# Queues of VectorE and ScalarE in order of use, in all stages of seven products, and the second sums of weights behind the first splits

## The chip, the core and the metric

The kernel runs on one core of one Trainium2 chip. The metric is the device time of one execution in microseconds. TensorE (PE) multiplies, VectorE (DVE), ScalarE (ACT) and GpSimd (POOL) prepare operands and take results away, SyncE (SP) issues most of the loads. Each engine works through its own queue in the order in which the program put its instructions there, and waits on semaphores for the others.

## What is computed

One decoder layer for 512 tokens of width 2048 in float32: an input projection shared by three groups of heads, the heads themselves, an output projection, and a feed-forward layer of width 8192.

```python
xn = rms_norm(h, attn_norm_g)
proj = xn @ w_in
...
o = jnp.concatenate([gla_o, fox_o, mem_o], axis=2)
o = rms_norm(o, out_norm_g.reshape(N_OUT_HEADS, HEAD_DIM)).reshape(B, S, -1)
gate = jnp.concatenate([jax.nn.silu(gg), jax.nn.sigmoid(fg), jax.nn.sigmoid(mg)], axis=-1)
h = h + (o * gate) @ w_out

u = jax.nn.relu(rms_norm(h, mlp_norm_g) @ w_up)
h = h + (u * u) @ w_down
```

## The kernel before

**A product in float32.** Each operand is split into a high half in the type fp32r (ScalarE casts, `A.copy`) and a low half, the remainder (VectorE subtracts). `mm3` (L157 to L159) multiplies high by high, high by low and low by high.

**Seven products.** Part of the input projection and the whole output, up and down projections multiply blocks of two by two by the scheme with seven products in place of eight. `ORDER` is 1, 5, 6, 3, 7, 2, 4. Products 1, 2 and 3 take a raw block of the weight or one that is used as it was loaded, products 5, 6, 7 and 4 take sums of blocks. `multiply` (L337) runs the seven products for one set of weights (`Weights`). Of a set of the out, up and down stage each product has four steps q = 0 to 3 of 12 matmuls; a step is written (p, q) here. Of the input pairs (`Pair`) it has two steps. The out stage has two sets, up has eight groups, down has eight sets (four chunks of two).

**What a step needs.** `split(p, q)` makes the high and low half of 1024 columns of the weight, the tile `hl_..._pq`, in one of four buffers. At q = 0 it first calls `prepare` for both halves s of the block: the load of the next raw block (tiles `raw_..._rcs`, 2048 columns) by SyncE, and the sum of 2048 columns for products 5, 6, 7 and 4 by VectorE (in the input pairs GpSimd makes the sums of 7 and 4). So both sums of a product stand ahead of its first split. All that stands under a priority of `AHEAD`, and the scheduler places the instructions in the queues by it.

**Left operands.** `left0` to `left6` hold the seven sums of the activations, as high half (h) and low half (l; of S2 the last quarter is `left4m`). For the out stage, `gate(3)` makes the last quarter of these sums behind the attention heads: A11 and S1 are split at once (`left0`, `left3`), the others go through memory (`oo_i`) by GpSimd's DMAs and are loaded again by `fetch` and split by `resplit` (L1280). For down, `renew` loads and splits those of the next chunk while the current one runs.

**Evictions.** At the end of a product `after` takes the accumulators away, under the priority `urgent` (2 x AHEAD): in the input pairs into `o` (ScalarE L451 or VectorE L449), in out into `x` (VectorE L1217), in up into `z` (ScalarE copies L1356, or VectorE adds and ScalarE's relu L1316), in down into `m` (ScalarE L1400). From `z` the up stage makes transposes `ut` on TensorE (L1301) and squares `u` (L1302).

**First sets.** The weights of out0 and up0 are marked `lead`; their first eight steps run in the order (1,0), (1,1), (1,2), (5,0), (5,1), (5,2), (1,3), (5,3). `x_sums(0)` makes the sums of x for the input pairs from the tiles `xs`, and `qTs`, `kTs` (L373, L374) copy projections out of the banks in which `ss_x` (the sum of squares of x, L207) is then made.

## Time and profile before

| | us |
|---|---|
| median of 3 runs | 2146.14 (2144.59 to 2147.57) |
| the profiled execution | 2146.72 |
| its span | 2145.0 |

The stages of seven products lie in the span about so: input pairs 98 to 260 us, out 704 to 874, up 874 to 1517, down from 1517 to the end. Between the input pairs and out are the other projections and the heads. The granted clock of TensorE is 0.998 over the span.

A row of the profile names the engine, the line, the operation, the tile written and the tiles read (out<-in, buffer numbers left out), the shape, and for groups the count; "idle before" is the time for which the engine did nothing ahead of it, with what ended that.

### The profile page before, as it was taken

To read this page: it belongs to the slowest core of one execution; us is meant where nothing else is said; L and a number is where in the kernel's file an instruction comes from. 1 tells how busy PE (TensorE), PEld (TensorE's weight loads), DVE (VectorE), ACT (ScalarE), POOL (GpSimd) and SP (SyncE) were. 2 spreads that over 40 slices of the span, in tenths; PEclk is the share of its full clock that TensorE was granted. 3 is DMA by queue.
4 is the path that set the end of the run, shared out by engine and by line. 5 is a ranking of instruction groups with operands and counts; after the bars stand their busy time and mean duration, and the time that the engine had idled before them with its cause. 6 is when DMAs were issued, how large, how long until landed. Compare 5 with 4: busy or idle time off the path is not lost.

```text
span 2145.0 us, 25543 instructions
## 1 busy us (share of the span) xinstructions
PE 2104.4 (98%) x9746; PEld 1732.6 (81%) x9746; DVE 1615.4 (75%) x1723; ACT 1134.3 (53%) x1603; POOL 191.7 (9%) x236
## 2 busy tenths in 40 slices
PE   8999999999999899999999999999999999999999
PEld 7877778887888788788888888888788788788787
DVE  7679897773664988977777777778867767877875
ACT  6554464434554655655555555556546546556543
POOL 0252200000000021100000000000100000000000
PEclk9999999999999999999999999999999999999999
DMA  7544342121233675253353353356578568668653
GB/s 264 168 138 139 98 149 85 60 69 59 84 105 136 230 268 205 92 196 128 135 192 128 141 189 132 134 190 232 170 203 245 159 192 258 170 183 276 174 166 130
DMA packets 78755, 347.09 MB, mean 162 GB/s; under 512 B 9305, under 2 KB 13401, under 8 KB 57130
## 3 DMA queue, kind: packets, MB, share of 16 engines
q1 hardware_dynamic: 58778, 274.95, 36.9%
q0 software_dynamic: 19856, 70.53, 12.5%
q8 instruction: 76, 1.25, 0.2%
q14 instruction: 45, 0.37, 0.1%
HBM read 271.52 MB, written 73.92 MB: 161 GB/s over the span
## 4 chain that ended last, share of the span: by engine, by line
PE 80%; DVE 9%; DMA 6%; issue 3%; ACT 2%; POOL 1%; SPq 0%; ACTq 0%; DVEq 0%; POOLq 0%
PE acc_up L157 9%; PE acc_up L158 9%; PE acc_up L159 9%; PE acc_dn L158 7%; PE acc_dn L159 7%; PE acc_dn L157 7%; PE acc_out L158 2%; PE acc_out L157 2%; PE acc_out L159 2%; DMA left1l<-op 2%; DVE hl_dn L334 2%; PE gg L157 1%; PE gg L159 1%; PE gg L158 1%; DVE raw_dn L296 1%
## 5 line engine op out<-in xcount | busy, mean ns | idle before, releaser
L334 DVE TENSOR_TENSOR hl_up<-raw_up,hl_up 128x1024 fp32r<-128x1024 f32 x224 | 271.6, 1222 | 142.7 <-ACT hl_up L334 142.5
L334 ACT CAST hl_up<-raw_up 128x1024 fp32r<-128x1024 f32 x224 | 235.7, 1054 | 254.0 <-PE acc_up L159 194.0
L334 DVE TENSOR_TENSOR hl_dn<-raw_dn,hl_dn 128x1024 fp32r<-128x1024 f32 x224 | 270.5, 1222 | 103.9 <-ACT hl_dn L334 103.3
L334 ACT CAST hl_dn<-raw_dn 128x1024 fp32r<-128x1024 f32 x224 | 235.0, 1055 | 206.5 <-PE acc_dn L159 164.5
L296 DVE TENSOR_TENSOR raw_dn<-raw_dn,raw_dn 128x2048 f32<-128x2048 f32 x64 | 146.1, 2287 | 15.1 <-DMA raw_dn<-in_w_down_dram 14.9
L296 DVE TENSOR_TENSOR raw_up<-raw_up,raw_up 128x2048 f32<-128x2048 f32 x64 | 145.1, 2267 | 2.0 <-DMA raw_up<-in_w_up_dram 1.9
L1401 POOL DMA_DIRECT2D hd<-m x48 | 41.6, 866 | 514.4 <-ACT m L1400 514.4
L334 ACT CAST hl_out<-raw_out 128x1024 fp32r<-128x1024 f32 x56 | 58.6, 1053 | 52.8 <-PE acc_out L159 40.1
L334 DVE TENSOR_TENSOR hl_out<-raw_out,hl_out 128x1024 fp32r<-128x1024 f32 x56 | 69.0, 1253 | 15.1 <-ACT hl_out L334 15.0
L1400 ACT COPY m<-acc_dn 128x512 f32<-128x512 f32 x96 | 54.6, 587 | 31.8 <-PE acc_dn L159 31.8
L1293 POOL DMA_DIRECT2D op<-u x32 | 17.1, 535 | 491.5 <-ACT u L1302 484.1
L158 PE MATMUL acc_dn<-hl_dn,left 128*128 128x512 f32 x128 | 50.3, 393 | 6.1 <-DVE hl_dn L334 6.1
L158 PE MATMUL acc_in<-hl_hl_in,sh 128*128 128x512 f32 x128 | 50.5, 395 | 5.4 <-DVE hl_hl_in L334 5.4
L157 PE MATMUL acc_up<-hl_up,left 128*128 128x512 f32 x128 | 50.6, 396 | 3.1 <-ACT z L1356 3.1
L157 PE MATMUL gg<-ahi_x,hl_gg 128*128 128x512 f32 x128 | 53.6, 418 | 0.0
L334 DVE TENSOR_TENSOR hl_hl_in<-spare,hl_hl_in 128x1024 fp32r<-128x1024 f32 x31 | 44.0, 1430 | 11.5 <-ACT hl_hl_in L334 11.4
L157 PE MATMUL acc_in<-hl_hl_in,sh 128*128 128x512 f32 x128 | 50.0, 390 | 1.3 <-ACT o L451 1.3
L158 PE MATMUL acc_dn<-hl_dn,left0h 128*128 128x512 f32 x128 | 50.0, 391 | 1.1 <-DVE hl_dn L334 1.1
L334 ACT CAST hl_hl_in<-spare 128x1024 fp32r<-128x1024 f32 x31 | 32.4, 1049 | 34.8 <-DVE spare L430 14.6
L157 PE MATMUL acc_up<-hl_up,left0h 128*128 128x512 f32 x128 | 50.5, 394 | 0.0
L157 PE MATMUL acc_up<-hl_up,left5h 128*128 128x512 f32 x128 | 50.5, 394 | 0.0
L157 PE MATMUL acc_up<-hl_up,left1h 128*128 128x512 f32 x128 | 50.5, 394 | 0.0
(545 smaller groups left out, 6277.1 us busy)
## 6 DMA issues: line engine op xcount, KB each, us to landing
raw_up<-in_w_up_dram SPq DMA_DIRECT2D x64, 1024.0 KB, 4.9
raw_dn<-in_w_down_dram SPq DMA_DIRECT2D x64, 1024.0 KB, 6.3
hd<-m POOLq DMA_DIRECT2D x48, 512.0 KB, 5.5
raw_out<-in_w_out_dram SPq DMA_DIRECT2D x16, 1024.0 KB, 5.3
op<-u POOLq DMA_DIRECT2D x32, 512.0 KB, 3.3
op<-s POOLq DMA_DIRECT2D x24, 512.0 KB, 3.5
spare<-in_w_pair_dram SPq DMA_DIRECT2D x16, 512.0 KB, 4.2
raw_in<-in_w_pair_dram SPq DMA_DIRECT2D x16, 512.0 KB, 4.3
```

Of the source, the lines that this page charges most:

```text
L157: T.matmul(ps, lhsT=ah, rhs=bh, start=start, stop=False, skip_group_check=on)
L158: T.matmul(ps, lhsT=ah, rhs=bl, start=False, stop=False, skip_group_check=on)
L159: T.matmul(ps, lhsT=al, rhs=bh, start=False, stop=stop, skip_group_check=on)
L296: V.tensor_sub(dst, a, b)
L334: made = A.copy(hi, part), V.tensor_sub(lo, part, hi.bitcast(F32))
L1293: nc.gpsimd.dma_start(down_op[c][i][:, half * 1024 : half * 1024 + 1024], tile)
L1400: A.copy(st[:, t * 512 : t * 512 + 512], acc[t])
L1401: nc.gpsimd.dma_start(dst, st.rearrange("p (t n) -> p t n", t=2), accum_op=ALU.add)
```

## The change

`turns["step"]` counts the steps. `empty` places an eviction under the high priority and remembers the last instruction of it on VectorE and on ScalarE; `behind(step)` puts what is issued in it behind the evictions up to that step. A split is now placed behind the evictions of four steps before, and behind the split that was made before it (`turns["made"]`), so splits stand in their order of use. `prepare` falls into `load_next` (both loads, at q = 0) and `sums`: the sum for half s is placed at q = s, that is, the second directly before split q = 1, and behind the evictions of eight steps before. The first sum of product 7 follows the last split of 5, that of 4 the last split of 7.

In the lead sets the sums of product 6 are cut into four pieces of 1024 columns, each before its split. For out0 the left operands that were loaded again are split at given steps (`in_turn`), in pieces of 512 or 1024 columns in the same chain as the weights. `gate(3)` gives its sums in three parts with different priorities, and its temporary tiles have other tags (buffers). In up0 the normalisation `rstd` is computed at step (6, 1), not (1, 1).

```diff
 
-    turns = dict(group=0, hl=0, raw=0)
+    turns = dict(group=0, hl=0, raw=0, step=0, made=())
+
...
+    def empty(evict, p, acc):
+        traced = nc.cur_bb.bb.instructions
+        last = traced[-1]
+        with tc.high_priority(offset=2 * AHEAD):
+            evict(p, acc)
+        start = next(i for i in reversed(range(len(traced))) if traced[i] is last) + 1
+        for engine in (V.engine, A.engine):
+            emptied.extend([(turns["step"], i) for i in traced[start:] if i.engine == engine][-1:])
+
+    def behind(step):
+
+        es = ExitStack()
+        for engine in (V.engine, A.engine):
+            for _, i in [e for e in emptied if e[0] <= step and e[1].engine == engine][-1:]:
+                es.enter_context(tc.issue_after(i))
+        return es
     spare = third.tile([128, 3584], F32, tag="third", name="spare")
...
-        def prepare(self, p, s):
+        def load_next(self, p):
+            if p in (1, 5, 6, 2):
+                to, r, c = {1: (self.t, 0, 0), 5: (self.b12, 0, 1), 6: (self.b22, 1, 1), 2: (self.b21, 1, 0)}[p]
+                to.extend([self.load(r, c, s) for s in range(2)])
+
+        def sums(self, p, s):
             t, b12, b22, b21 = self.t, self.b12, self.b22, self.b21
-            if p == 1:
-                t.append(self.load(0, 0, s))
-            elif p == 5:
-                b12.append(self.load(0, 1, s))
+            if p == 5:
                 cs = slice(0, 1024 if self.lead and s else self.per * 1024)
                 self.minus(p, t[s][:, cs], b12[s][:, cs], t[s][:, cs])
-            elif p == 6:
-                b22.append(self.load(1, 1, s))
+            elif p == 6 and not self.lead:
                 self.minus(p, t[s], b22[s], t[s])
             elif p == 7:
                 self.minus(p, b12[s], b22[s], b12[s])
-            elif p == 2:
-                b21.append(self.load(1, 0, s))
             elif p == 4:
                 self.minus(p, t[s], b21[s], t[s])
...
+            now = turns["step"]
             with tc.high_priority(offset=self.ahead if urgent else AHEAD):
                 if q == 0:
-                    for s in range(2):
-                        self.prepare(p, s)
+                    self.load_next(p)
+                if q < 2:
+                    with behind(now - 8) as es:
+                        last = (p, 0) if q else {7: (5, self.steps - 1), 4: (7, self.steps - 1)}.get(p)
+                        if self.lead and (p, q) == (7, 0):
+                            last = 6, 3
+                        if last:
+                            es.enter_context(tc.issue_after(self.parts[last][2][1].ins))
+                        self.sums(p, q)
                 blocks = {1: self.t, 5: self.t, 6: self.t, 4: self.t, 3: self.b22, 7: self.b12, 2: self.b21}[p]
                 raw = blocks[q // self.per]
-                if self.lead and (p, q) == (5, 3):
-                    cs = slice(1024, 2048)
-                    V.tensor_sub(raw[:, cs], self.b12[1][:, cs], raw[:, cs])
+                if self.lead and (p == 6 or (p, q) == (5, 3)):
+                    cs = slice(q % 2 * 1024, q % 2 * 1024 + 1024)
+                    b = self.b12 if p == 5 else self.b22
+                    with ExitStack() as es:
+                        if p == 6:
+                            es.enter_context(tc.issue_after((self.parts[6, q // 3][2][1] if q else seam[0]).ins))
+                        V.tensor_sub(raw[:, cs], b[q // 2][:, cs], raw[:, cs])
                 both = self.both(f"hl_{self.name}_{p}{q}")
                 hi, lo = both[:, :1024], both[:, 1024:]
                 at = q % self.per * 1024
                 part = raw[:, at : at + 1024]
-                made = A.copy(hi, part), V.tensor_sub(lo, part, hi.bitcast(F32))
+                with behind(self.first + 6 if self.lead and p == 6 else now - 4) as es:
+                    for i in turns["made"]:
+                        es.enter_context(tc.issue_after(i.ins))
+                    turns["made"] = made = A.copy(hi, part), V.tensor_sub(lo, part, hi.bitcast(F32))
             self.parts[p, q] = hi, lo, made
             return hi, lo, made
...
         chain = {}
+        w.first = turns["step"] + 1
         for p, q in steps:
+            turns["step"] += 1
             first = p in (1, 5, 2)
...
             if q == w.steps - 1:
-                after(p, acc)
+                with ExitStack() as es:
+                    if w.lead and p == 5:
+                        es.enter_context(tc.issue_after(seam[1].ins))
+                    after(p, acc)
 
...
     def in_pair(n, c):
+        def evict(p, acc):
+            r, col = WHERE[p]
+            for u in range(2):
+                t = 2 * r + u
+                dst = o[:, t, n * 1024 + col * 512 : n * 1024 + col * 512 + 512]
+                if c or p in (3, 7, 2):
+                    V.scalar_tensor_tensor(dst, acc[u], rs_x(t), dst, op0=ALU.mult, op1=ALU.add)
+                else:
+                    A.activation(dst, acc[u], AF.Copy, scale=rs_x(t))
+
         def after(p, acc):
-            r, col = WHERE[p]
-            with urgent():
-                for u in range(2):
-                    t = 2 * r + u
-                    dst = o[:, t, n * 1024 + col * 512 : n * 1024 + col * 512 + 512]
-                    if c or p in (3, 7, 2):
-                        V.scalar_tensor_tensor(dst, acc[u], rs_x(t), dst, op0=ALU.mult, op1=ALU.add)
-                    else:
-                        A.activation(dst, acc[u], AF.Copy, scale=rs_x(t))
+            empty(evict, p, acc)
...
         def temp(v):
-            tags = dict(s1="tb" if last else "bT", s2="td", s3="tb" if last else "eb", s4="td")
...
-        for i, src in block_sums(ot[:, :2, :256], ot[:, 2:, :256], ot[:, :2, 256:], ot[:, 2:, 256:], temp):
...
+        def keep_sums():
+            for i, src in block_sums(ot[:, :2, :256], ot[:, 2:, :256], ot[:, :2, 256:], ot[:, 2:, 256:], temp):
+                early = i in (A11, S1) or i == S2 and not last
+                if early and high:
+                    hi, lo = halves(high[i][:, cs]), halves(lower(i, cs))
+                    A.copy(hi, src)
+                    seam[:] = [V.tensor_sub(lo, src, hi.bitcast(F32))]
+                else:
+                    nc.gpsimd.dma_start(halves(out_op[i][:, cs]), src)
+                    if early:
+                        waiting.append((i, cs))
+                if i in (S2, S4):
+                    yield
...
+
+        sums = keep_sums()
+        next(sums)
+        return sums
 
     def place():
 
...
+    with tc.high_priority(offset=AHEAD):
+        next(sums)
+    with tc.high_priority(offset=AHEAD - 150):
+        next(sums)
 
...
                 nc.sync.dma_start(z[r, c].rearrange("p (t n) -> p t n", t=2), x[r, 2 * n + c])
 
+        def evict(p, acc):
+            for t in range(2):
+                v = z[WHERE[p]][:, t * 512 : t * 512 + 512]
+                V.tensor_add(v, v, acc[t])
+
         def after(p, acc):
             r, c = WHERE[p]
-            with urgent():
-                for t in range(2):
-                    v = z[r, c][:, t * 512 : t * 512 + 512]
-                    V.tensor_add(v, v, acc[t])
+            empty(evict, p, acc)
...
         def inside(p, q):
+            if not n and (p, q) == (5, 3):
+                first_operands()
+            if not n and p == 6 and q < 3:
+                w_first.split(3, q)
+                if q != 1:
+                    in_turn(S4, slice(512, 1536) if q == 0 else slice(1536, 2048))
+            if not n and q > 1 and p in (3, 7, 2):
+                for cs in ((slice(1024, 1536), slice(1536, 2048)) if q > 2 else (slice(0, 1024),)):
+                    in_turn({3: S3, 7: A12, 2: A22}[p], cs)
...
+    def in_turn(i, cs):
+
+        with ExitStack() as es:
+            es.enter_context(tc.high_priority(offset=AHEAD))
+            for m in turns["made"]:
+                es.enter_context(tc.issue_after(m.ins))
+            turns["made"] = split_left(i, cs, lower(i, cs).bitcast(F32))
+
+    def first_operands():
+        for q in range(4):
+            if q == 3:
+                in_turn(S2, slice(1536, 2048))
+            _, _, made = w_first.split(6, q)
+        seam.append(made[1])
+        in_turn(S4, slice(0, 512))
+
     def rest():
...
             with tc.high_priority(offset=1000):
                 fetch(i, cs, out_op[i][:, cs])
-            resplit(i, cs)
     for n in range(2):
         out_pair(n)
...
         def after(p, acc):
-            with urgent():
-                evict(p, acc)
+            empty(evict, p, acc)
...
                 rest()
-            if not g and (p, q) == (1, 1):
+            if not g and (p, q) == (6, 1):
```

The first place is ScalarE's queue between the copies of the query projection and the first input pair. `xs_1_951` and `xs_0_966` are the tiles xs_12_1 and xs_13_0 of x, `hl_hl_in_50` and `_51` splits (5,0) and (5,1). Before:

```order
L374 ACTIVATE qTs<-gq_111 128x4x128
L374 ACTIVATE qTs<-gq_112 128x4x128
L374 ACTIVATE qTs<-gq_113 128x4x128
L391 ACTIVATE xs_1_951<-xs_1_951,colt 128x512
L334 CAST hl_hl_in_51_1041<-spare 128x1024
L120 ACTIVATE y_x<-s_x 128x4
L374 ACTIVATE qTs<-gq_114 128x4x128
L391 ACTIVATE xs_0_966<-xs_0_966,colt 128x512
```

and after:

```order
L429 ACTIVATE xs_1_951<-xs_1_951,colt 128x512
L429 ACTIVATE xs_0_966<-xs_0_966,colt 128x512
L412 ACTIVATE qTs<-gq_111 128x4x128
L412 ACTIVATE qTs<-gq_112 128x4x128
L412 ACTIVATE qTs<-gq_113 128x4x128
L367 CAST hl_hl_in_51_1041<-spare 128x1024
L120 ACTIVATE y_x<-s_x 128x4
L412 ACTIVATE qTs<-gq_114 128x4x128
```

Both scalings of x tiles moved ahead of all four copies into qTs.

The second place is VectorE's queue in the first out set, from split (5,3) or the evictions of product 1 on. `x_00` and `x_11` are the residual blocks into which products 1 and 5 are evicted, `raw_out_00s` the raw blocks of which the sums for product 6 are made. Before:

```order
L334 TENSOR_TENSOR hl_out_53_5986<-raw_out_001_5744,hl_out_53_5986 128x1024
L334 TENSOR_TENSOR hl_out_60_6009<-raw_out_000_5742,hl_out_60_6009 128x1024
L296 TENSOR_TENSOR raw_out_001_5744<-raw_out_111_6006,raw_out_001_5744 128x2048
L334 TENSOR_TENSOR hl_out_61_6026<-raw_out_000_5742,hl_out_61_6026 128x1024
L296 TENSOR_TENSOR raw_out_010_5915<-raw_out_110_6003,raw_out_010_5915 128x2048
L1217 TENSOR_TENSOR x_00_5887<-x_00_5887,acc_out_1_0_5873 128x512
L1217 TENSOR_TENSOR x_00_5887<-x_00_5887,acc_out_1_1_5874 128x512
L1217 TENSOR_TENSOR x_11_5936<-x_11_5936,acc_out_5_0_5913 128x512
L1217 TENSOR_TENSOR x_11_5936<-x_11_5936,acc_out_5_1_5914 128x512
L334 TENSOR_TENSOR hl_out_62_6041<-raw_out_001_5744,hl_out_62_6041 128x1024
L334 TENSOR_TENSOR hl_out_63_6056<-raw_out_001_5744,hl_out_63_6056 128x1024
L296 TENSOR_TENSOR raw_out_011_5918<-raw_out_111_6006,raw_out_011_5918 128x2048
```

and after, from the first eviction:

```order
L1267 TENSOR_TENSOR x_00_5869<-x_00_5869,acc_out_1_0_5855 128x512
L1267 TENSOR_TENSOR x_00_5869<-x_00_5869,acc_out_1_1_5856 128x512
L367 TENSOR_TENSOR hl_out_60_5988<-raw_out_000_5742,hl_out_60_5988 128x1024
L359 TENSOR_TENSOR raw_out_000_5742<-raw_out_110_5983,raw_out_000_5742 128x1024
L359 TENSOR_TENSOR raw_out_001_5744<-raw_out_111_5985,raw_out_001_5744 128x1024
L367 TENSOR_TENSOR hl_out_61_5992<-raw_out_000_5742,hl_out_61_5992 128x1024
L359 TENSOR_TENSOR raw_out_001_5744<-raw_out_111_5985,raw_out_001_5744 128x1024
L367 TENSOR_TENSOR hl_out_62_5996<-raw_out_001_5744,hl_out_62_5996 128x1024
L582 TENSOR_TENSOR left4m<-left4m,left_5031 128x512
L367 TENSOR_TENSOR hl_out_63_6002<-raw_out_001_5744,hl_out_63_6002 128x1024
L1267 TENSOR_TENSOR x_11_5917<-x_11_5917,acc_out_5_0_5895 128x512
L1267 TENSOR_TENSOR x_11_5917<-x_11_5917,acc_out_5_1_5896 128x512
```

The evictions of product 1 moved ahead of split (6,0), split (5,3) is further ahead (five instructions stand between it and this piece), the sums of product 6 stand in pieces between its splits, the sum for product 7 (`raw_out_010`) has moved behind, and the low half of left4m stands before split (6,3).

The third place is ScalarE's queue at the first down set. `z_7_11396` (after: `z_7_11408`) is z4 of the last up group, `u_12` the square of its transpose, `hl_dn_0_pq` the splits. Before:

```order
L542 CAST left1h<-left1l 128x1024
L334 CAST hl_dn_0_12_11457<-raw_dn_0_001_11408 128x1024
L334 CAST hl_dn_0_13_11472<-raw_dn_0_001_11408 128x1024
L334 CAST hl_dn_0_50_11504<-raw_dn_0_000_11406 128x1024
L542 CAST left2h<-left2l 128x1024
L334 CAST hl_dn_0_51_11519<-raw_dn_0_000_11406 128x1024
L542 CAST left2h<-left2l 128x1024
L334 CAST hl_dn_0_52_11534<-raw_dn_0_001_11408 128x1024
L334 CAST hl_dn_0_53_11549<-raw_dn_0_001_11408 128x1024
L1316 ACTIVATE z_7_11396<-acc_up_1_0_10840,rstd 128x512
L1316 ACTIVATE z_7_11396<-acc_up_1_1_10841,rstd 128x512
```

and after:

```order
L582 CAST left1h<-left1l 128x1024 x2
L367 CAST hl_dn_0_12_11469<-raw_dn_0_001_11420 128x1024
L1394 ACTIVATE z_7_11408<-acc_up_1_0_10852,rstd 128x512
L1394 ACTIVATE z_7_11408<-acc_up_1_1_10853,rstd 128x512
L367 CAST hl_dn_0_13_11484<-raw_dn_0_001_11420 128x1024
L367 CAST hl_dn_0_50_11515<-raw_dn_0_000_11418 128x1024
L582 CAST left2h<-left2l 128x1024
L367 CAST hl_dn_0_51_11531<-raw_dn_0_000_11418 128x1024
L1380 ACTIVATE u_12_11452<-ut_12_0_11453 128x4x128
L1380 ACTIVATE u_12_11452<-ut_12_1_11459 128x4x128
L582 CAST left2h<-left2l 128x1024
```

The relu of z4 moved ahead of splits (1,3) and (5,0) and of both casts of left2, and the square of its transpose ahead of left2's second cast.

More of the change, by code (lines that the diff above doesn't have):

```diff
@@ L1127, in projections @@
             assert n in heads_of
[L1128 removed]
+            for _ in gate(n, ps):
+                pass
             yield
```

24 lines of the change are left out of this document (7 added, 17 removed).

## The prediction

> **What bounds the kernel now.** I read the page's shares first.
>
> ```profile
> span 2145.0 us, 25543 instructions
> PE 2104.4 (98%) x9746; PEld 1732.6 (81%) x9746; DVE 1615.4 (75%) x1723; ACT 1134.3 (53%) x1603; POOL 191.7 (9%) x236
> ```
>
> TensorE is busy 98% of the span. The change leaves its matmuls and transposes as they are, so it can win only what TensorE waits for, and what a wait does to the next matmuls. The view of waits, for TensorE, lists them all; these are the rows of the stages of seven products and of what stands around them (us in total, times, longest):
>
> ```profile
> PE acc_dn L158 <- DVE hl_dn L334: 7.3, 6, 1.8
> PE acc_in L158 <- DVE hl_hl_in L334: 5.4, 5, 1.5
> PE acc_up L157 <- ACT z L1356: 3.1, 1, 3.1
> PE acc_out L157 <- DVE x L1217: 3.1, 1, 3.1
> PE ut L1301 <- ACT z L1316: 2.7, 1, 2.7
> PE acc_out L158 <- DVE hl_out L334: 2.2, 2, 1.8
> PE acc_out L157 <- ACT left3h L1080: 1.9, 1, 1.9
> PE acc_in L157 <- ACT o L451: 1.3, 1, 1.3
> PE ss_x L207 <- ACT qTs L374: 1.1, 1, 1.1
> PE acc_in L157 <- DVE o L449: 0.7, 1, 0.7
> ```
>
> They add up to 28.8 us in some twenty places. Waits on the low half of a split (L158 <- DVE) come to 14.9 us; the others are waits for an eviction or for one operand, each once.
>
> A long wait costs more than itself: the granted clock falls behind it. The view by windows (us, PE busy, granted clock, DMA share, GB/s) shows the place:
>
> ```profile
> 728.00:734.00 6.00, 4.15 (x10) 0.72 0.72 234
> 734.00:743.00 9.00, 7.55 (x27) 0.81 0.97 349
> 902.30:905.70 3.40, 3.40 (x9) 0.50 0.00 0
> ```
>
> A window's length times the clock that is missing gives the loss: 6 x 0.28, 9 x 0.19 and 3.4 x 0.50, about 1.7 us each, 5.1 us in all. So **33.9 us** (28.8 + 5.1) is the most that the change can win in these stages, 1.6%.
>
> How far the splits run ahead elsewhere tells whether the steady part has anything to lose. From the page's costliest groups, and one whole group of the up stage from the windows:
>
> ```profile
> L334 ACT CAST hl_up<-raw_up 128x1024 fp32r<-128x1024 f32 x224 | 235.7, 1054 | 254.0 <-PE acc_up L159 194.0
> L334 DVE TENSOR_TENSOR hl_up<-raw_up,hl_up 128x1024 fp32r<-128x1024 f32 x224 | 271.6, 1222 | 142.7 <-ACT hl_up L334 142.5
> L296 DVE TENSOR_TENSOR raw_up<-raw_up,raw_up 128x2048 f32<-128x2048 f32 x64 | 145.1, 2267 | 2.0 <-DMA raw_up<-in_w_up_dram 1.9
> ```
>
> The casts there stand idle 194.0 us until TensorE frees one of four buffers, and VectorE idles 142.5 us for the casts: TensorE is the slowest of the three and the splits lean on their buffers. A step of TensorE is
>
> ```profile
> 720.67 0.39 PE L159 MATMUL acc_out<-hl_out,left3l 128*128 128x512 f32 x1
> ...
> 723.39 0.39 PE L159 MATMUL acc_out<-hl_out,left0l 128*128 128x512 f32 x1
> ```
>
> 12 matmuls later, 2.72 us. With four buffers a cast starts three steps ahead of its use, 8.2 us; less the cast (1.05) and the subtraction (1.22) the lead is at best 5.9 us.
>
> **The change, part by part.** The same instructions are issued but for 8 more on VectorE and 4 more on ScalarE, because some sums and operand splits are cut into pieces. Two pieces of 1024 columns take 2.35 us on VectorE where one of 2048 takes 2.28 (rows in (b)), so a cut adds about 0.07 us, nothing that counts. What matters is who stands before whom. I go by place.
>
> *(a) Input products, 98 to 260 us: +2.7 us.* On ScalarE two scalings of the x tiles, xs_12_1 and xs_13_0, now stand ahead of the copies qTs, for the first of which the statistics matmul ss_x waits.
>
> ```profile
> 93.88 1.59 ACT L391 ACTIVATE xs<-xs,colt 128x512 f32<-128x512 f32 x2 [6.17 <-DMA xs<-in_xT_dram]
> 96.31 1.56 ACT L374 ACTIVATE qTs<-gq 128x512 f32<-128x512 f32 x3
> 94.64 0.43 DVE L244 TENSOR_TENSOR st<-xs,xs 128x256 f32<-128x256 f32 x1 [2.60 <-ACT xs L391]
> 97.05 1.02 PE L207 MATMUL ss_x<-wide,xacc 128*128 128x1 f32 x8 [1.12 <-ACT qTs L374]
> DMA to landing us min/median/max: 2.8/3.4/3.6
> ```
>
> The two tiles take buffers that VectorE's sums of the tiles before them must release. The new order runs those four sums in a row from 94.64, 0.34 us each, so the last buffer is free at 96.0. The loads land 2.8 to 3.6 us later (98.8 to 99.6), the two scalings take 0.73 us each, qTs starts at 100.1 to 101.1 in place of 96.31, and ss_x follows 0.74 us behind it: +3.8 to +4.8, I take +4.1. Queued behind the two blocked scalings on ScalarE is, besides qTs, the cast of split (5,1), which TensorE needs only later. TensorE is then idle from about 95.9 to 101.2, longer than the wait ahead of the 0.50 window, so I add 1.3 us of slow clock (the idle time takes part of that window itself). Against this, TensorE arrives some 5 us later at everything behind, where VectorE, GpSimd and the evictions are not pushed back as far: the waits of 1.3 (o by ScalarE), 0.7 (o by VectorE) and the first of the five on a split (1.5) go, 3.5 us. Of the other four I expect +0.8, as GpSimd's second difference now stands before split (5,1) of the second pair. 4.1 + 1.3 - 3.5 + 0.8 = +2.7. Bounds: 0 (everything absorbed) and +5.5 (nothing).
>
> *(b) Output products, first pair, 704 to 760 us: -3.3 us.*
>
> ```profile
> 709.46 1.23 DVE L296 TENSOR_TENSOR raw_out<-raw_out,raw_out 128x1024 f32<-128x1024 f32 x1 [1.79 <-DMA raw_out<-in_w_out_dram]
> 721.09 0.68 DVE L1069 TENSOR_TENSOR o<-o,ee_mg 128x512 f32<-128x512 f32 x1
> 721.70 2.28 DVE L296 TENSOR_TENSOR raw_out<-raw_out,raw_out 128x2048 f32<-128x2048 f32 x1
> 723.90 1.29 DVE L244 TENSOR_TENSOR s_mg<-o 128x512 f32<-128x512 f32 x2
> 726.91 2.35 DVE L334 TENSOR_TENSOR hl_out<-raw_out,hl_out 128x1024 fp32r<-128x1024 f32 x2
> 734.72 2.47 DVE L1217 TENSOR_TENSOR x<-x,acc_out 128x512 f32<-128x512 f32 x4
> 737.40 0.62 ACT L542 CAST left<-left4m 128x512 fp32r<-128x512 f32 x1 [3.86 <-DMA left4m<-oo]
> ```
>
> Now: the whole 2048-wide difference at 721.70 and the gate's sums stand before split (5,3), which ends at 728.0; the evictions into x start at 734.72 behind five splits and sums. That is 1.9 + 1.8 + 3.1 of waits and 3.4 of slow clock, 10.0 us with TensorE. After: gate products fill VectorE's idle 1.79 us at 709.46, worth about 1.65 us; the step behind 721.70 then begins at 720.05 and runs gate sum (0.60), split (5,3) (1.14), left3l and a gate sum (1.20), half a difference (1.14), two gate sums, two evictions (2.40), split (6,0) (1.14): it ends at 727.7. Step (5,3) starts without a wait at 723.6 and ends at 726.3, so (6,0) waits 1.2 us at its second matmul. (6,1) has two half differences and a split before it, 3.4 us against a step of 2.72: 0.7. Before (6,3) the new queues of both engines put the cast and the low half of left4m, whose load landed at 737.40 here; if it lands between 735 and 737.4 (the store it needs comes no earlier, but the queue ahead of it changed), (6,3) waits 1.7 to 2.9 us: 2.3. VectorE is saturated, with the eviction of x_01 now ahead of (7,0): 2.5 for (7,0) and (7,1). New sum 6.7, gain 3.3. Bounds: 0 and 6.
>
> Here a rule of the Trainium skill can be held against the trace. The row 902.30:905.70 shows half clock for 3.4 us behind a wait of 3.1 us. The Trainium skill, "TensorE: Matmul & The Clock Gate", section "What's actually happening", says that the clock drops to half after at least one idle window of about 3.4 us and comes back after about 3.4 us of work. The length agrees with the row; the threshold doesn't, since a wait of 3.1 us, and two of 1.9 and 1.8 us in a row, sufficed. By the page none of the new waits of (b) would slow the clock and the term stays -3.3; by the trace a pair of them can, and it would be -1.6.
>
> *(c) Up products, first group, 890 to 906 us: -2.4 us.*
>
> ```profile
> 898.28 1.99 ACT L334 CAST hl_up<-raw_up 128x1024 fp32r<-128x1024 f32 x2 [3.82 <-DVE raw_up L296]
> 900.18 2.04 ACT L1356 COPY z<-acc_up 128x512 f32<-128x512 f32 x4
> 899.23 0.68 DVE L543 TENSOR_TENSOR left4m<-hs,left 128x512 fp32r<-128x512 f32 x1
> 899.83 1.22 DVE L334 TENSOR_TENSOR hl_up<-raw_up,hl_up 128x1024 fp32r<-128x1024 f32 x1
> 874.00:900.00 26.00, 23.59 (x107) 18.96 (x105) 26.00 (x23) 15.80 (x23) 0.55 (x1) 1.00 0.07 28
> ```
>
> The copies of z stood behind two casts that waited 3.82 us for a difference on VectorE, and TensorE waited for z until 900.81: 3.1 + 1.7 of clock, 4.8 us. After, the copies come first. Late is then the low half of (6,0): at 901.05 before, less half a difference (1.06) and left4m (0.60): 899.4 against TensorE's stop at 897.7, 1.7 us. (6,1) waits 0.7 more, since VectorE has no gap here (26.00 of 26.00 us in the last row). Gain 2.4; bounds 1 and 4.
>
> *(d) Down products, 1516 us to the end: -9.2 us.*
>
> ```profile
> 1525.23 1.06 ACT L542 CAST left2h<-left2l 128x1024 fp32r<-128x1024 f32 x1 [3.04 <-DMA left2l<-op]
> 1530.84 1.26 ACT L1316 ACTIVATE z<-acc_up,rstd 128x512 f32<-128x512 f32 x2
> 1534.35 4.49 DVE L296 TENSOR_TENSOR raw_dn<-raw_dn,raw_dn 128x2048 f32<-128x2048 f32 x2
> ```
>
> The last relu of the up stage (1530.84) stood behind casts of left1 and left2 that waited for loads (3.04 us), and the transposes ut waited 2.7 us for it. After, it stands ahead of left2's casts and the transposes come later: 2.7 go. Split (6,0) stood behind two differences of 4.49 us; two fewer stand before it now, one of these and one ahead of them, so its 1.8 us go. The other 5.5 us are the same place in later chunks: a cast of left1 waits for its load while a weight split stands behind it. It now follows split (1,3), so the load has some two steps more (5.4 us), against waits of at most 1.8. I leave 0.8 us for what is late next: 10.0 - 0.8 = 9.2. Bounds: 6 and 10.
>
> *(e) All other groups: 0.* Each split now may wait for the evictions four steps back and for the split before it in order of use, and one sum (2.20 us) stands directly before the second split of products 5, 6, 7 and 4. The lead of up to 5.9 us covers this: the densest stretch, from behind split (5,0) through (6,1), is four sums (8.8) and five splits (5.7), 14.5 us in five steps of TensorE (13.6), so it eats 0.9 us, and 2.1 where an eviction of 2 x 0.60 falls in.
>
> **Sum.** +2.7 - 3.3 - 2.4 - 9.2 + 0 = -12.2. The profiled execution took 2146.72 us itself (span 2145.0), 0.6 above the median of the runs: 2146.7 - 12.2 = **2134.5 us**. Adding the bounds, the far ends are -20 (0, -6, -4, -10) and -1.5 (+5.5, 0, -1, -6): 2126.7 to 2145.2.
>
> **The rivals.**
>
> 1. *The seams give the gain back* (0.10). Both new waits are real: ss_x is late by 5.5 with nothing absorbed, and in (b) VectorE is the bound, so that order only moves the wait. Then the far end holds, -1.5: 2145.2. For it: VectorE has no gap in (c) and hardly one in (b). Against it: (d), the largest term, has VectorE idle elsewhere and doesn't depend on it.
>
> 2. *All waits go* (0.06): VectorE's filled gaps pull all of (b) and (c) early, ss_x is absorbed. 10.0 + 4.8 + 10.0 = 24.8 less: 2122. Against it: VectorE's saturation, and two tiles that ScalarE must now wait for.
>
> 3. *The lead is eaten; slower* (0.08). In the 16 weight sets that aren't a first one of their stage (one in out, seven in up, eight in down), the stretch (5,0) to (6,1) starts with a lead of 0.5 us only, because the evictions and the chaining in order hold the splits back. Then 2.1 - 0.5 = 1.6 us is lost per set, 16 x 1.6 = 26 us: 2134.5 + 26 = 2160. It decides where the lead at (5,0) is below 2.1 us; it has 5.9 at best, and the casts' 194.0 us of idle time for TensorE speak against it.
>
> 4. *The change doesn't do what it says* (0.04): where an engine is saturated, queue order changes nothing that ends last, and only (d)'s 2.7 and 1.8 go, against +2.7 in (a): 2145.
>
> The forecast, from -20 to about -4.4, keeps 0.72.
>
> **How the numbers follow.** A change under 0.2% (4.3 us) is about what a measurement of this kernel can't tell from none. Faster: the forecast and rival 2, 0.78. Same: rivals 1 and 4, 0.14. Slower: rival 3, 0.08. The range 2126.7 to 2145.2 takes in the forecast and rivals 1 and 4, less some tails, about 0.82.
>
> **What would show each step.** (a) the wait of ss_x for qTs grows from 1.1 to about 5 us, with a granted clock below 1.00 behind it, and the first split wait of acc_in and both waits on o are gone. (b) left3h and the 3.1 us on x are gone; waits on hl_out or left4 around (6,0) to (7,1) add up to some 7 us. (c) the wait on z is gone, hl_up appears with about 2.4 us. (d) ut <- z is gone and acc_dn <- hl_dn falls from 7.3 to about 1. (e) no new rows in acc_up and acc_dn with counts near 16. The prediction is wrong if rows with such counts appear, if a DMA becomes the releaser in the up or down stage, or if ss_x isn't late.

## The result, and the profile after

The changed kernel takes 2135.2 us (median of 4 runs, 2134.73 to 2135.82) against 2145.67 us (4 runs): a ratio of 0.9949, interval 0.9937 to 0.9961. The profiled execution took 2135.63 us itself, span 2133.9, against 2146.72 before: 11.1 us less, where 12.2 had been forecast.

The page's shares after:

```profile
span 2133.9 us, 25579 instructions
PE 2103.5 (99%) x9746; PEld 1734.1 (81%) x9746; DVE 1620.9 (76%) x1731; ACT 1134.4 (53%) x1607; POOL 195.7 (9%) x236
```

TensorE is busy for the same 2104 us; what went is its idle time. The view of waits for TensorE after (us in total, times, longest; three rows from outside these stages, the same size before, are left out):

```profile
PE ss_x L226 <- ACT qTs L412: 7.3, 1, 7.3
PE acc_in L177 <- DVE hl_hl_in L367: 4.0, 4, 2.6
PE acc_out L177 <- DVE hl_out L367: 2.6, 5, 0.8
PE acc_out L176 <- ACT hl_out L367: 1.4, 1, 1.4
PE acc_dn L177 <- DVE hl_dn L367: 1.3, 4, 0.3
PE acc_up L176 <- ACT hl_up L367: 1.0, 1, 1.0
PE acc_up L177 <- DVE hl_up L367: 0.8, 1, 0.8
PE acc_out L176 <- DVE x L1267: 0.3, 1, 0.3
```

Five kinds of wait have gone: on z in up, on z ahead of the transposes ut, on left3h, and on o by either engine; of the 3.1 us on x 0.3 are left. The down stage's 7.3 us on splits are 1.3. One wait grew by much: ss_x for qTs, 1.1 to 7.3 us. Three rows are new: a cast in out (1.4 us), and a cast and a low half in up (1.0 and 0.8 us). No row has a count near 16.

The first matmul of each stage in the timeline gives the stages' lengths in us (the last column to the end of TensorE's last matmul):

| kernel | to out | out | up | down |
|---|---|---|---|---|
| before | 704.6 | 169.9 | 643.3 | 623.0 |
| after | 708.1 | 166.7 | 641.7 | 613.2 |
| difference | +3.6 | -3.2 | -1.6 | -9.8 |
| forecast | +2.7 | -3.3 | -2.4 | -9.2 |

The granted clock, from the view by windows of after (us, PE busy, clock, DMA share, GB/s), shows what else was lost:

```profile
98.00:108.00 10.00, 5.77 (x20) 0.50 0.40 133
100.00:110.00 10.00, 7.77 (x28) 0.59 0.31 97
740.00:750.00 10.00, 7.80 (x27) 0.83 0.72 287
899.00:904.00 5.00, 4.24 (x12) 0.66 0.00 0
1516.00:1600.00 84.00, 84.00 (x377) 1.00 0.65 185
```

The last row is the seam into the down stage, where two waits of 2.7 and 1.8 us stood before: TensorE runs through it, 84.00 of 84.00 us. In the others the clock still falls behind a wait. Longest around ss_x: it is at half for all of 98 to 108 us, and TensorE works in 5.77 us of them, so it costs 5.77 x 0.50 = 2.9 us there.

### The profile page after: what moved, and what is told of

Its sections match the earlier page's. It is cut to its first block, busy times and chain, and to the rows that moved or that the text cites. A ratio compares the mean times of both kernels' runs of the same rounds, so it can differ in the third digit from the quotient of the medians.

```text
span 2133.9 us, 25579 instructions
## 1 busy us (share of the span) xinstructions
PE 2103.5 (99%) x9746; PEld 1734.1 (81%) x9746; DVE 1620.9 (76%) x1731; ACT 1134.4 (53%) x1607; POOL 195.7 (9%) x236
## 4 chain that ended last, share of the span: by engine, by line
PE 89%; DMA 4%; DVE 4%; ACT 2%; issue 1%; SPq 0%; POOL 0%; ACTq 0%; DVEq 0%; POOLq 0%
PE acc_dn L177 9%; PE acc_dn L178 9%; PE acc_dn L176 9%; PE acc_up L177 9%; PE acc_up L178 9%; PE acc_up L176 9%; PE acc_out L177 2%; PE acc_out L178 2%; PE acc_out L176 2%; PE acc_in L177 2%; PE acc_in L178 2%; PE acc_in L176 2%; PE gg L176 1%; PE gg L178 1%; PE gg L177 1%; DMA xs<-in_xT_dram 1%
## 5 line engine op out<-in xcount | busy, mean ns | idle before, releaser
L315 DVE TENSOR_TENSOR raw_up<-raw_up,raw_up 128x2048 f32<-128x2048 f32 (+1 forms) x62 | 140.6, 2268 | 0.0
L1394 ACT ACTIVATE z<-z,rstd 128x512 f32<-128x512 f32 x48 | 32.2, 717 | 44.8 <-DVE z L1443 44.8
L177 PE MATMUL acc_in<-hl_hl_in,sh 128*128 128x512 f32 x128 | 50.3, 393 | 4.0 <-DVE hl_hl_in L367 4.0
L176 PE MATMUL acc_up<-hl_up,left 128*128 128x512 f32 x128 | 50.4, 395 | 1.0 <-ACT hl_up L367 1.0
L177 PE MATMUL acc_up<-hl_up,left 128*128 128x512 f32 x128 | 50.5, 395 | 0.8 <-DVE hl_up L367 0.8
```

Of the source, the lines that this page charges most:

```text
L176: T.matmul(ps, lhsT=ah, rhs=bh, start=start, stop=False, skip_group_check=on)
L177: T.matmul(ps, lhsT=ah, rhs=bl, start=False, stop=False, skip_group_check=on)
L315: V.tensor_sub(dst, a, b)
L1394: A.activation(dst, src, AF.Relu, scale=rstd[:, 2 * row + t : 2 * row + t + 1])
```

## The experiments

Each kernel is the changed one with the edit shown, unless said otherwise. Ratios are to the kernel before on the same chip. A single edit of 3 us is a difference of 0.0015 between ratios, about the half width of one interval (0.0012 to 0.0018); what settles a place is therefore its waits and its stage's length in the trace, with the medians beside.

**1. qTs ahead of the x tiles.**

```diff
                 nc.sync.dma_start(a, xT[k])
-                A.activation(a, a, AF.Copy, scale=g_attn[:, k : k + 1])
+                with ExitStack() as es:
+                    if c and (j == 3 or j == 2 and a is a2):
+                        es.enter_context(tc.issue_after(q_copies[2].ins))
+                    A.activation(a, a, AF.Copy, scale=g_attn[:, k : k + 1])
```

(`q_copies` are the four copies into qTs.)

> After with one edit: the last three scalings of x tiles on ScalarE (xs_12_1, xs_13_0, xs_13_1) are held until the third copy into qTs has been issued. Theory (order on ScalarE alone makes ss_x late): its wait falls from 7.3 us to 1 to 2 us and the slow clock behind it goes, so the first input product starts some 6 us earlier; of that, the waits that had been absorbed (1.3, 0.7 and 1.5 us) come back, net -3 us, 2132. Rival (nothing had been absorbed): the whole 6 us stay, 2129. Second rival (ss_x waits for the loads anyway): no change, 2135.

Measured: 2132.12 us, ratio 0.9934 (0.9921 to 0.9948). After has this chain on ScalarE and TensorE (timeline: start, length, engine, operation, idle time before it and what ended that):

```profile
99.91 0.72 ACT L429 ACTIVATE xs<-xs,colt 128x512 f32<-128x512 f32 x1 [3.28 <-DMA xs<-in_xT_dram]
100.88 0.72 ACT L429 ACTIVATE xs<-xs,colt 128x512 f32<-128x512 f32 x1 [0.26 <-DMA xs<-in_xT_dram]
101.51 1.55 ACT L412 ACTIVATE qTs<-gq 128x512 f32<-128x512 f32 x3
102.23 1.84 PE L226 MATMUL ss_x<-wide,xacc 128*128 128x1 f32 x8 [7.34 <-ACT qTs L412]
DMA to landing us min/median/max: 3.6/4.0/4.9
```

ScalarE sits at the scalings until their loads land, and qTs, which has nothing to do with those loads, waits in the queue. (The last row is from the view of the tile xs: the loads took 3.6 to 4.9 us, against 2.8 to 3.9 before in the same window.) With the edit the view of waits says:

```profile
PE ss_x L226 <- ACT qTs L413: 1.9, 1, 1.9
PE acc_in L177 <- DVE hl_hl_in L367: 5.0, 4, 2.6
PE acc_in L176 <- DVE o L490: 0.3, 1, 0.3
```

5.4 us of ss_x's wait are gone, 1.3 us of the absorbed waits come back, and out starts at 705.6, 2.6 us earlier. The order on ScalarE is the cause, and the loss is partly absorbed, as the theory had it. Of the clock's part 1.7 of 2.9 us stayed (0.83 over 96 to 106 us, behind a wait of 1.9), and the clock fell once more at the second input pair: 0.88 over 186 to 200 us, 1.7 us, where it is 1.00 in after. The first input product starts 6.0 us earlier and out only 2.6; the 1.3 us of waits and these 1.7 us are most of the difference.

**2. Both sums before the first split again** (outside the first sets of out and up).

```diff
-                if q < 2:
+                for s in range(2) if not q and not self.lead else [q] if self.lead and q < 2 else []:
                     with behind(now - 8) as es:
...
-                        self.sums(p, q)
+                        self.sums(p, s)
```

> After with one part undone: in all sets but the first of out and up, both sums of a product stand before its first split again; evictions and the order of the splits stay as in after. Theory (evictions and splits in order carry most of the gain in the down stage, the late second sums only the 1.8 us of split (6,0) and a little elsewhere): +2 to +4 us in down, and about -3 in the input pairs, where the x tiles fall behind qTs again: 2134 to 2136. Rival (the late sums carry the down stage): +8 in down, 2140. Second rival (they carry nothing): 2132.

Measured: 2134.57 us, ratio 0.9946 (0.9934 to 0.9959). The view of waits and one window:

```profile
PE acc_dn L177 <- DVE hl_dn L367: 5.1, 4, 2.1
PE acc_in L177 <- DVE hl_hl_in L367: 5.5, 5, 1.6
PE acc_in L176 <- ACT o L488: 1.3, 1, 1.3
1688.00:1697.00 9.00, 6.88 (x24) 0.81 0.37 58
```

The down stage takes 618.3 us, 5.1 more than after: 3.8 us of waits and 1.7 of clock (9 x 0.19), together 5.5. Out starts at 703.1, 5.0 earlier than in after: without the late second sums the x tiles never overtake qTs. So the late sums give some 5 us in down and are at the same time what costs in the input pairs. The total is inside the theory's range, but both of its parts are larger than I had put them and cancel. Evictions and splits in order do not carry most of the down stage's gain, as the theory had it.

**3. Splits not held.**

```diff
-                with behind(self.first + 6 if self.lead and p == 6 else now - 4) as es:
-                    for i in turns["made"]:
+                with ExitStack() as es:
+                    for i in turns["made"] if self.lead else ():
```

> After with another part undone: splits of weights are held neither behind the evictions of four steps before nor (outside the first sets) behind the split before; the late sums and the priority of evictions stay. Theory (the hold matters only where ScalarE has casts ready before z, that is in the first up group): the wait on z there comes back, +1 to +3 us, nothing in down: 2136 to 2138. Rival (the hold carries the down stage): +8, 2143. Second rival (no part): 2135.

Measured: 2135.8 us, ratio 0.9951 (0.9938 to 0.9963). The total is 0.2 us under the range that I expected, and the place is another:

```profile
PE acc_out L176 <- DVE x L1267: 7.3, 1, 7.3
PE acc_up L176 <- ACT z L1433: 0.6, 1, 0.6
PE acc_dn L177 <- DVE hl_dn L367: 1.4, 3, 0.8
```

The wait on z in the first up group is only 0.6 us, and up takes 638.7 us, 3.0 *less* than in after. In out the wait on x is back, 7.3 us in one piece: without the hold, the sums and splits of product 6 stand ahead of the evictions again, and out takes 169.1 us, 2.4 more than after. Down takes 613.7 us as in after. So the hold pays in the first out set, costs in the first up group, and does nothing for down beside the late sums.

**4. left4m behind split (6,3).**

```diff
         for q in range(4):
+            _, _, made = w_first.split(6, q)
             if q == 3:
                 in_turn(S2, slice(1536, 2048))
-            _, _, made = w_first.split(6, q)
```

> After with one pair swapped: in the first out set the split of left4m stands behind weight split (6,3), not ahead of it, on both engines. Theory (the weight's cast queues behind a cast that waits for a load): of the two waits at step (6,3), 1.6 and 1.0 us over the usual pace, 1 to 2 us go, and the slow clock behind them (1.1) with it if they fall short enough: -1.0 to -3.0 us, 2132 to 2134. Rival (VectorE is the bound there and the wait moves to a later step): 2135.

Measured: 2132.42 us, ratio 0.9931 (0.9918 to 0.9943). Out takes 164.8 us, 1.9 less. In after (timeline of ScalarE):

```profile
740.64 0.62 ACT L582 CAST left<-left4m 128x512 fp32r<-128x512 f32 x1 [5.29 <-DMA left4m<-oo]
741.17 1.04 ACT L367 CAST hl_out<-raw_out 128x1024 fp32r<-128x1024 f32 x1
```

and with the edit (timeline of ScalarE, then two rows of the waits):

```profile
735.14 1.06 ACT L367 CAST hl_out<-raw_out 128x1024 fp32r<-128x1024 f32 x1 [1.37 <-DVE raw_out L359]
739.04 0.62 ACT L582 CAST left<-left4m 128x512 fp32r<-128x512 f32 x1 [2.84 <-DMA left4m<-oo]
PE acc_out L176 <- ACT hl_out L367: 0.5, 1, 0.5
PE acc_out L176 <- ACT left L582: 0.5, 1, 0.5
```

The weight's cast now runs 3.9 us ahead of left4m's instead of behind it. At (6,3) TensorE waits only for left4m's cast, 0.5 us in place of 2.2, and the clock stays at 1.00 over 736 to 750 us. The other row is at product 7, where the waits rose from 0.7 to 1.3 us. The rest of the lower median is not of this place: ss_x waited 4.4 us in the profiled execution, with the order of after.

**5. rstd behind split (6,3)** of the first up group.

```diff
-            if not g and (p, q) == (6, 1):
-                ss = const.tile([128, NT], F32, name="ss_h")
...
+            if not g and (p, q) == (6, 3):
+                with tc.issue_after(w.parts[6, 3][2][1].ins):
+                    ss = const.tile([128, NT], F32, name="ss_h")
...
```

> After with one edit: in the first up group the sum of squares and the five small steps of the normalisation rstd stand behind split (6,3), not ahead of split (6,0), on VectorE and ScalarE. Theory (they hold split (6,0) up by about 1 us on ScalarE and VectorE): the 1.0 us wait for the cast of (6,0) goes, the 0.8 us of (6,1) stays, and the slow clock behind (1.7 us) goes if the two together were needed for it: -1.0 to -2.7 us, 2132.5 to 2134. Rival (the copies of z ahead of the cast set its time, not rstd): no change, 2135.

Measured: 2129.8 us, ratio 0.9931 (0.9918 to 0.9943). After has, on ScalarE and VectorE (timelines):

```profile
896.17 0.20 ACT L120 ACTIVATE y_h<-s_h 128x4 f32<-128x4 f32 x1 [3.27 <-DVE s_h L119]
896.52 1.05 ACT L1433 COPY z<-acc_up 128x512 f32<-128x512 f32 x2
897.46 1.05 ACT L367 CAST hl_up<-raw_up 128x1024 fp32r<-128x1024 f32 x1
894.84 1.22 DVE L582 TENSOR_TENSOR left2l<-left2l,left2h 128x1024 fp32r<-128x1024 f32 x1
895.97 0.16 DVE L119 TENSOR_SCALAR s_h<-ss_h 128x4 f32<-128x4 f32 x1
```

Steps of 0.2 us for rstd wait 3.27 us for one of 0.16 us, which stands behind a split of left2 on VectorE; the copies of z and the cast of (6,0) queue behind them. With the edit the view of waits has one row left in up:

```profile
PE acc_up L177 <- DVE hl_up L367: 0.2, 1, 0.2
```

Up takes 638.6 us, 3.1 less than in after: 1.6 us of waits, and the clock, which is now 1.00 over 890 to 904 us. The 0.8 us, which I had put down to (6,1) and expected to stay, went too; under (c) below the trace shows that it was the low half of (6,0). For the rest of the median's 5.4 us, ss_x waited only 3.4 us in this execution and out started 2.4 us earlier.

**6. No hold in the first up group alone.**

```diff
-                with behind(self.first + 6 if self.lead and p == 6 else now - 4) as es:
+                with behind(now - 99 if self.name == "up0" else self.first + 6 if self.lead and p == 6 else now - 4) as es:
```

> After with the hold behind evictions taken off the splits of product 6 in the first up group alone (casts (6,0) to (6,2) move ahead of the copies of z). The run with free splits everywhere was 3.0 us quicker than after in the up stage. Theory (that is this place: the hold makes the cast wait for z): the waits of 1.0 and 0.8 and the slow clock go, a wait on z of some 0.6 comes: -3 us, 2132. Rival (the quicker up stage came from the other groups or from a phase of the clock): -0.5 to 0, 2135.

Measured: 2131.44 us, ratio 0.9938 (0.9925 to 0.9950). Up takes 639.2 us, 2.5 less than in after, with one wait, on z:

```profile
PE acc_up L176 <- ACT z L1433: 1.0, 1, 1.0
```

So the quicker up stage of experiment 3 did come from this place. Experiment 5 shows that the hold itself was not the cost: with it kept and rstd out of the way, up takes 638.6 us. That this is 0.6 us better still shows nothing: the unedited up stage took 640.7 to 641.8 us in four executions.

**7. Both undone.** The edit of 2, and that of 3 outside the first sets.

> After with two parts undone together outside the first sets: both sums of a product ahead of its first split, and splits neither held behind evictions nor chained. What stays of the change is the seam of the first out set, the first up group and the priority of evictions. Theory (late sums or the hold, either of them, put z and the split of (6,0) in time in the down stage, and only with both undone does all of it go): the down stage loses the 9.8 us that it had won, the input pairs win 3 to 5: 2140 to 2142. Rival (half of the down gain comes from something else): 2135 to 2137.

Measured: 2135.47 us, ratio 0.9953 (0.9940 to 0.9965). Down takes 620.9 us: 7.7 of its 9.8 us are lost.

```profile
PE acc_dn L177 <- DVE hl_dn L367: 5.1, 3, 2.2
1534.00:1542.00 8.00, 6.70 (x22) 0.79 0.44 68
1688.00:1697.00 9.00, 6.80 (x23) 0.81 0.25 32
```

Two waits of over 2 us at the first splits of product 6 of a chunk are back, each with a slowed clock (8 x 0.21 and 9 x 0.19 us, 3.4 together). The 2.7 us on z ahead of the transposes did not come back, though neither part stood. The total missed the theory's 2140 to 2142, because the stage up to out took 702.5 us, 5.6 less than in after, more than the 3 to 5 that I had added for it, and up took 640.4, 1.3 less. It lies in the rival's 2135 to 2137, but not by the rival's reason: far more than half of the down stage's gain went. Which part of the change moved that z ahead in down stays open. It is not the priority of evictions, which I had listed as a part: the kernel before has it too (2 x AHEAD). Both this run and that of experiment 2 keep the sums behind the evictions of eight steps before, and the sums of products 7 and 4 behind the last splits of 5 and 7; no run undid those.

**8. Three edits together.** Those of 1, 4 and 6:

> After with three edits together: the x tiles held behind qTs, left4m behind split (6,3), no hold in the first up group. Theory (three places apart in time, each on TensorE's path): the gains add, -3.1 - 2.8 - 3 = -8.9, 2126. Rival (they share the same slow clock or what one wins is waited for at the next seam): half of it, 2131.

Measured: 2127.32 us, ratio 0.9921 (0.9906 to 0.9936). Then those of 1, 4 and 5:

> After with three edits together: the x tiles held behind qTs, left4m behind split (6,3), rstd behind split (6,3). Theory (three separate places; the medians of the single runs stand 3.1, 2.8 and 5.4 us below after): between 2126 (places add by their own waits: 3.1 + 2.8 + 3) and 2124 (by the medians), with at most 0.2 us of waits left in the up stage. Rival (the single medians hold chance differences of when loads land): not below the earlier run of three edits, 2127.

Measured: 2126.23 us, ratio 0.9905 (0.9887 to 0.9922). And with the sums of the input pairs early, in place of the edit of 1:

```diff
-                if q < 2:
+                for s in range(2) if self.steps == 2 and not q else [q] if self.steps > 2 and q < 2 else []:
```

> After with three edits: both sums of a product ahead of its first split in the input pairs alone (out, up and down keep the late ones), left4m behind split (6,3), rstd behind split (6,3). Theory (the late second sum is what let the x tiles overtake qTs, and GpSimd's late second difference is the 2.6 us wait of the second pair): ss_x waits about 1 us, no split wait of the input pairs is over 1.7 us, the input pairs end about 5 us ahead of after and 1.5 ahead of before: 2124 to 2126. Rival (holding the x tiles alone is enough, the waits come to the same sum): 2127.

Measured: 2126.05 us, ratio 0.9903 (0.9887 to 0.9919). The waits of the second of the three:

```profile
PE ss_x L226 <- ACT qTs L413: 0.5, 1, 0.5
PE acc_in L177 <- DVE hl_hl_in L367: 5.9, 5, 2.6
PE acc_in L176 <- DVE o L490: 1.7, 1, 1.7
PE acc_up L177 <- DVE hl_up L367: 0.2, 1, 0.2
```

The three places add: in the profile of the second, the stages up to out, out and up are 2.2, 2.4 and 3.0 us shorter than in after, where the single edits of 1, 4 and 5 gave 2.6, 1.9 and 3.1. All three kernels beat both before and after; their intervals do not touch that of after. Early sums in the input pairs and held x tiles come to the same total. In the third, ss_x waited 1.8 us and splits of the pairs still 4.8, up to 2.4, and out started at 705.0, 0.4 us behind before and not 1.5 ahead of it: what I had expected of GpSimd's difference there did not show.

**9. The changed kernel once more.**

> The changed kernel itself once more, with no edit, on the same chip as the two others. Five runs with the same order around qTs (after, and four of its variants) showed a wait of ss_x of 2.9 to 7.3 us. Theory (the wait is the landing of two loads, which differs from execution to execution): again a value between 3 and 7.3, and a time of 2133 to 2136 that follows it. Rival (7.3 is fixed and the variants changed something ahead of it): 7.3 again.

Measured: 2134.12 us, ratio 0.9948 (0.9932 to 0.9963), and

```profile
PE ss_x L226 <- ACT qTs L412: 5.4, 1, 5.4
PE acc_dn L177 <- DVE hl_dn L367: 2.9, 7, 0.8
```

With the same queue order, ss_x waited 2.9, 3.4, 4.4, 5.4, 5.8 and 7.3 us in six executions; the wait of the changed kernel's first profile was the longest of them. The theory's two loads are not where the spread lies: from the start of the last sum that frees their buffers to qTs it is 5.1 to 5.4 us in all six (timelines of VectorE and ScalarE). That sum itself starts between 92.1 and 96.1 us, so the spread comes from the x tiles ahead, whose scalings also wait for loads.

Nor did the time follow the wait. This execution took 2138.30 us, 2.7 more than the first profile, with 1.9 less on ss_x: the clock was at half for 8.6 us of work around ss_x (0.51 over 99.0 to 109.5 us) and fell once more at the second input pair (0.83 over 190 to 200 us), so out started 0.3 us later, and down took 615.7 us, 2.5 more. With the down stage of after unedited, nine executions took 611.9 to 615.9 us there. The 618.3 and 620.9 us of experiments 2 and 7 lie outside this spread, but what the late sums are worth is known to about 2 us only.

## Why the prediction was right

**The sum.** -12.2 was forecast for the profiled execution, -11.1 measured, by the places that were named. Several sizes were off, and some of these errors cancel.

(a) +2.7 forecast, +3.6 measured. That ss_x would wait for qTs behind two scalings, that the clock would fall, and that later waits would absorb part of it, is what the traces show. All three sizes were too small: ss_x starts 5.2 us later (102.23 against 97.05), where I had 4.1, because the last buffer came free at 96.6 and not 96.0, and the loads took 3.6 to 4.9 us where I had 2.8 to 3.6; the slow clock cost 2.9 us, where I had 1.3; and 4.5 us of these 8.1 come back by the start of out, where I had 2.7. The waits show 3.4 of them (2.0 on o, 1.4 on splits); the 0.8 us that I had added for GpSimd's difference did not come in sum. That errors of 1.1, 1.6 and 1.8 us leave 0.9 is luck. The wait of some 5 us that I named is the middle of the six executions, not the 7.3 of the profile.

(b) -3.3 against -3.2. (What I took off, 1.9 + 1.8 + 3.1 + 3.4, is 10.2, not 10.0.) left3h and all but 0.3 of the 3.1 on x went; for x experiment 3 shows the hold as the cause, for left3h the order is the only argument, as no run undid the gate's earlier sums. (6,3) waited for the cast that queues behind left4m (1.44 + 0.76 us; 2.3 forecast); experiment 4 shows the cause. Of the 2.5 us for (7,0) and (7,1) 0.7 came; in place of the rest the clock fell (10 x 0.17 = 1.7 us) behind (6,3). Two errors cancel here. The paragraph on the clock had named this loss, and left it out of the sum.

(c) -2.4 against -1.6. The wait on z went. I had named the low half of (6,0) as late next, at 1.7 us, and 0.7 for (6,1). After (timelines of TensorE and VectorE):

```profile
898.57 0.50 PE L176 MATMUL acc_up<-hl_up,left 128*128 128x512 f32 x1 [0.95 <-ACT hl_up L367]
899.83 0.62 PE L177 MATMUL acc_up<-hl_up,left 128*128 128x512 f32 x1 [0.76 <-DVE hl_up L367]
898.55 1.23 DVE L367 TENSOR_TENSOR hl_up<-raw_up,hl_up 128x1024 fp32r<-128x1024 f32 x1 [1.15 <-ACT hl_up L367]
```

Both waits are at (6,0), for its cast and then for its low half, which VectorE could only make behind the cast: 0.95 + 0.76 = 1.7 us, the size that I had. But neither the half difference nor left4m held it; the cast was late, with rstd's small steps as the cause, which I had not seen (experiment 5). (6,1) did not wait. The step that I had wrong is the clock: it stayed slow (5 x 0.34 = 1.7 us), where I had it gone.

(d) -9.2 against -9.8. The seam is clean. Experiments 2 and 7 show that the late second sums carry about half of it, and that with the splits free as well 7.7 us of it are lost. The 2.7 us on z went with every variant. For the later chunks I had named casts of left1 that wait for their loads. The rows nearest to the waits show the reason of the first chunk again: three of them, 1.45, 1.47 and 1.45 us, are at split (6,0), whose cast waits for a difference on VectorE. In the second chunk, before:

```profile
1700.72 1.05 ACT L334 CAST hl_dn<-raw_dn 128x1024 fp32r<-128x1024 f32 x1 [2.46 <-DVE raw_dn L296]
1701.80 0.50 PE L158 MATMUL acc_dn<-hl_dn,left 128*128 128x512 f32 x1 [1.45 <-DVE hl_dn L334]
```

In after, left1's casts of that chunk still wait 3.48 us for their load, and splits wait 0.6 us there. With early sums (experiment 2) waits of 1.89, 2.12, 0.24 and 0.81 us came back at the four chunks' (6,0): in the first two chunks the late sums are the cause, in the other two that is not shown.

(e) 0 against 0. Rival 3, the lead eaten, did not come: up is quicker by 1.6 us, and 1.3 us is all that splits of the down stage still wait for.

Rival 1 was half right: ss_x was late by over 5 us, but (b) gave nothing back. Rival 2 (2122) is what the kernels of experiment 8 come nearer to, with 2126, once the seams of (a), (b) and (c) are mended.

## What to carry to other kernels

An operation that waits for a load makes all that stands behind it in its engine's queue wait for that load: put operands that are ready ahead of it, and place small steps that feed something late (rstd here) behind the work that is needed now. In the down stage, placing each second sum just before its use was worth more than keeping splits behind evictions; in the input pairs it cost as much again. Moving a sum reorders what a scheduler places around it, so look at every seam for what overtook what. A stall that is cut to half can cost its clock all the same, so count both.

## What the runs showed of the hardware that I had not expected

In after, two waits of 1.0 and 0.8 us, 1.3 us apart, went with a drop of the clock (0.66 in the window 899 to 904); with one wait of 1.0 us at that place (experiment 6), or none (experiment 5), it stayed at 1.00. The waits alone do not decide it. In the execution of experiment 4 the same two waits left the clock at 1.00 over 890 to 905 us, and at the second input pair a wait of 2.56 us left it at 1.00 in after (186 to 200 us) and not in experiment 1 (0.88). What else decides is open.

In the last kernel of experiment 8 a wait of 1.8 us at ss_x was enough, with twelve matmuls of a single column behind it:

```profile
97.05 1.02 PE L226 MATMUL ss_x<-wide,xacc 128*128 128x1 f32 x8 [1.76 <-ACT qTs L412]
96.00:106.00 10.00, 8.95 (x39) 0.83 0.36 105
```

At 0.5 us (the second kernel there) the clock stayed full, and so it did before, at 1.1 us. The Trainium skill, "TensorE: Matmul & The Clock Gate", section "What's actually happening", asks for an idle window of about 3.4 us. These traces don't agree: the clock fell behind waits of 1.0 and 0.8 us, and behind one of 1.8. The same section of the Trainium skill has the clock back after about 3.4 us of sustained work. The drops in out and up agree, with 1.7 us lost at each, half of 3.4; the one around ss_x doesn't, where TensorE worked 5.77 us at half clock in the first profile and 8.6 us in that of experiment 9.
